# Gate and up projections: one low-half weight tile per chunk made by ScalarE and an accumulating DMA instead of VectorE

## Chip, cores and metric

The kernel runs on one core of one Trainium2 chip. The metric is device time in microseconds (us) from start to end of one execution. Three runs of the kernel before gave 1091.05, 1091.73 and 1091.93 us, a median of 1091.73 us. The execution that the profile shows is another one: it took 1091.39 us, of which 1089.6 us are the span from the first to the last instruction of the program; the other 1.79 us lie around it.

## What is computed

The reference is an encoder trunk of two layers on 256 tokens of width 1024, all in float32. One layer:

```
x = x + 0.5 * swiglu(rms_norm(x, ffn1_norm), w_gate, w_up, w_down)      # ffn 1
h = rms_norm(x, mix_norm);  z = h @ w_in                                # mix: two attention branches
x = x + merged(attention branches, gates) @ w_out
x = x + 0.5 * swiglu(rms_norm(x, ffn2_norm), w_gate, w_up, w_down)      # ffn 2

def swiglu(x, w_gate, w_up, w_down):
    return (silu(x @ w_gate) * (x @ w_up)) @ w_down
```

The hidden width of the feed-forward part (ffn) is 2816. There are four ffn in all, two in each layer, and each has its own weights.

## The kernel before

**Float32 accuracy by halves.** TensorE multiplies in a reduced format (`fp32r`). To keep float32 accuracy, each operand is split in a high half, which is the value rounded to fp32r, and a low half, which is the value minus the high half. A product is then three matmuls into the same PSUM bank: high by high, high by low and low by high. `three` (L167) issues them, on L168, L169 and L170: the second one is the first to read the low half of the weights.

**How weights arrive.** `load` (L137) takes a tile `raw` of 128 partitions by 1024 float32 (512 KB), issues a DMA for it on SyncE's queue (L140) and calls `parts` (L131), which takes a tile `wh` and a tile `wl` and lets `split_to` (L181) fill them: ScalarE copies `raw` to `wh` with the type fp32r (L182), then VectorE subtracts `wh` from `raw` into `wl` (L183). Three rings hold these tiles: `raw` has 4 buffers (RAW), `wh` and `wl` have 6 each (RING). A buffer is free again when its last reader is done: a `raw` after VectorE's subtraction, a `wh` or a `wl` after the last matmul that reads it.

**Gate and up.** The weights of gate and up lie interleaved, so that a chunk of 512 columns holds 256 gate columns and the 256 up columns that belong to them. `ffn` (L305) goes over 11 chunks (`NFC`, L434). For each, `columns` (L143) loads four tiles, each with two blocks of 128 rows out of the 1024 rows of the weights; the fourth tile holds the last 256 rows. Then, for each of the two halves `t` of the tokens, `project` (L270) runs 8 times `three`, that is 24 matmuls of 512 columns, over the four tiles in order. After it ScalarE takes the silu of the gate half (L447), VectorE multiplies it with the up half (`hh`, L449), and `defer` puts off the transposes of `hh` (`turn`, L312) for some matmuls. The first two chunks of the very first ffn are loaded in `opening` (L223) and are not made by the `columns` call of L441.

In a chunk, tile 4 is first read in the `t = 0` pass, after three quarters of its 24 matmuls, and last read at the end of the `t = 1` pass. With 6 buffers, a chunk's fourth `wl` takes the buffer of the second tile of the chunk before, if the buffers go round in turn; that one is given free halfway through the `t = 1` pass of the chunk before.

**Beside gate and up.** In chunks 2, 5 and 8, `prepare` (L357) builds sums of two rows of tiles for the down projection ahead of time: two more loads (L343), four subtractions (L347) and two more splits. `down` (L377) follows the 11 chunks, and after each first ffn of a layer stands `mix` (L470).

**Order of the work.** TensorE's order is written out by hand. The other engines' instructions are ordered at build time by the framework, from the program order and a simulated timeline, and each engine then runs its queue strictly in that order. GpSimd's queue (POOL) carries the reciprocal square roots of the norms (`rsqrt`, L172), the few loads of constants (L103 to L105, L461 to L468), and, in `mix` alone, attention work. The DMA issues of SyncE run on a queue of their own, in order.

Of the kernel before, what the change touches and what calls it, by code (L numbers as in the profile page):

```python
# [11 lines left out]
F32 = mybir.dt.float32  # L12
F32R = mybir.dt.float32r
I32 = mybir.dt.int32
BF16 = mybir.dt.bfloat16
AF = mybir.ActivationFunctionType
ALU = mybir.AluOpType
# [4 lines left out]
P = 128  # L22
D = 1024
# [4 lines left out]
KD = D // P  # L28
# [12 lines left out]
RING = 6  # L41
RAW = 4
# [14 lines left out]
def hybrid_encoder(ctx, tc, x, w_gu1, w_d1, w_in, b_gate, qk_gain, rpb, sink, t5,  # L57
                   w_bna, w_bsw, w_out, w_gu2, w_d2, c_mask, c_band, out):
    nc = tc.nc

    const = ctx.enter_context(tc.tile_pool(name="const", bufs=1))
    ring = ctx.enter_context(tc.tile_pool(name="ring", bufs=1))
# [68 lines left out]
    def parts(r, nk=2, n=512):  # L131
        wh = ring.tile([P, 2, 512], F32R, name="wh", tag="wh", bufs=RING)
        wl = ring.tile([P, 2, 512], F32R, name="wl", tag="wl", bufs=RING)
        split_to(wh[:, :nk, :n], wl[:, :nk, :n], r)
        return wh, wl

    def load(src, nk, n):  # L137
        raw = ring.tile([P, 2, 512], F32, name="raw", tag="raw", bufs=RAW)
        r = raw[:, :nk, :n]
        nc.sync.dma_start(r, src)  # L140
        return parts(r, nk, n)

    def columns(w, l, c0, n, nk=KD):  # L143
        return [load(w[l, 2 * i * P:(2 * i + 2) * P, c0:c0 + n].rearrange("(k p) n -> p k n", p=P), 2, n)
                for i in range(nk // 2)]

    def rows(w, l, k):
        return load(w[l, k * P:(k + 1) * P, :].rearrange("p (h n) -> p h n", h=2), 2, 512)
# [4 lines left out]
    def defer(lag, key, fn):  # L153
        later.append((now[0] + lag, len(later), key, fn))
        later.sort(key=lambda e: e[0])
# [25 lines left out]
    def split_to(hi, lo, src):  # L181
        linked("act", lambda: nc.scalar.activation(hi, src, AF.Copy))  # L182
        linked("dve", lambda: nc.vector.tensor_tensor(lo, src, hi.bitcast(F32), ALU.subtract))  # L183
# [39 lines left out]
    def opening(w, l):  # L223
        def piece(i, c=0):
            return load(w[l, 2 * i * P:(2 * i + 2) * P, c * 512:(c + 1) * 512].rearrange("(k p) n -> p k n", p=P),
                        2, 512)

        ps = [ps_g.tile([P, 512], F32, name="g", tag="g") for _ in range(T)]

        def steps(t, i):  # L230
            wh, wl = pieces[i]
            xh, xl = xT[t]
            for a, b in ((xh, wh), (xl, wh), (xh, wl)):
                for k in (2 * i, 2 * i + 1):
                    nc.tensor.matmul(ps[t], a[:, k, :], b[:, k % 2, :], start=a is xh and b is wh and k == 0,
                                     stop=b is wl and k == KD - 1)
            tick(2)

        pieces = []
        chain["act"] = warmed  # L240
        warmup(5)
        norm(0, 0, 0, True)
        pieces.append(piece(0))
        warmup(5)
        fetch(1, 0)
        norm(1, 0, 0, True)
        pieces.append(piece(1))
        fetch(0, 1)
        fetch(1, 1)
        warmup(3)  # L250
        steps(0, 0)
        norm(0, 0, 1, True)
        steps(1, 0)
        pieces.append(piece(2))
        norm(1, 0, 1, True)
        pieces.append(piece(3))
        square(0, 0, idle)
        square(0, 1, idle)
        second = [piece(0, 1)]
        square(1, 0, idle)  # L260
        square(1, 1, idle)
        second += [piece(i, 1) for i in range(1, KD // 2)]
        chain.clear()
        for i in (1, 2, 3):
            for t in range(T):
                steps(t, i)
        defer(24, "constants", constants)
        return ps, second

    def project(t, pieces, n):  # L270
        ps = ps_g.tile([P, 512], F32, name="g", tag="g")
        for k in range(KD):
            need(("norm", t, k // 4))
            xh, xl = xT[t]
            wh, wl = pieces[k // 2]
            three(ps[:, :n], xh[:, k, :], xl[:, k, :], wh[:, k % 2, :n], wl[:, k % 2, :n], k == 0, k == KD - 1)
            tick(n / 512)
        return ps
# [26 lines left out]
    def ffn(l, n, w_gu, w_d, after):  # L305
        with tc.tile_pool(name="ffn", bufs=1) as fp:
# [5 lines left out]
            def turn(c, t, hh):  # L312
                if t == 0:
                    tps[c] = ps_tp.tile([P, 4, P], F32, name="tp", tag="tp")
                tp = tps[c]
                for i in range(2):
                    nc.tensor.transpose(tp[:, SLOT[t][i], :], hh[:, i * P:(i + 1) * P], ident)  # L317
                if t < T - 1:
                    return
                m = 4 if PLAN[c] == "S" else 7  # L320
                hi = fp.tile([P, m, P], F32R, name=f"hi{m}", tag=f"hi{m}", bufs=NS if m == 7 else NFC - NS)
                lo = fp.tile([P, m, P], F32R, name=f"lo{m}", tag=f"lo{m}", bufs=NS if m == 7 else NFC - NS)
                if m == 7:
                    a = fp.tile([P, 8, P], F32, name="a", tag="sums", bufs=2)
                    nc.scalar.activation(a[:, :4, :], tp, AF.Copy)
                    for to, x, y, op in ((4, 0, 3, ALU.add), (6, 1, 0, ALU.subtract), (5, 4, 1, ALU.subtract),
                                         (7, 2, 5, ALU.subtract)):
                        nc.vector.tensor_tensor(a[:, to, :], a[:, x, :], a[:, y, :], op)
                    split_to(hi, lo, a[:, 1:, :])
                else:  # L330
                    with tc.high_priority(150 if c == NFC - 1 else 0):
                        split_to(hi, lo, tp)
                hs[c] = (hi, lo)
# [23 lines left out]
            def prepare(c):  # L357
                def into(name, r):
                    hl = [fp.tile([P, 2, 512], F32R, name=f"{name}{p}{c}", tag=f"{name}{p}{c}") for p in "hl"]
                    split_to(*hl, r)  # L360
                    return hl
                stored[c] = differences(block_row(2 * c), block_row(2 * c + 1), into)
# [71 lines left out]
            for c in range(NFC):  # L434
                first = n == 0 and c == 0
                if first:
                    both, second = opening(w_gu, l)
                elif n == 0 and c == 1:
                    pieces = second
                else:  # L440
                    pieces = columns(w_gu, l, c * 512, 512)  # L441
                if c in PREP:
                    prepare(PREP[c])
                for t in range(T):
                    ps = both[t] if first else project(t, pieces, 512)
                    sg = fp.tile([P, FC], F32, name="sg", tag="sg", bufs=2)
                    nc.scalar.activation(sg, ps[:, :FC], AF.Silu, scale=rstd[t])  # L447
                    hh = fp.tile([P, FC], F32, name="hh", tag="hh", bufs=2)
                    nc.vector.scalar_tensor_tensor(hh, ps[:, FC:], rstd[t], sg, op0=ALU.mult, op1=ALU.mult)  # L449
                    lag = LAST_LAG if (c, t) == (NFC - 1, T - 1) else H_LAG  # L450
                    defer(lag, ("h", c), lambda c=c, t=t, hh=hh: turn(c, t, hh))
# [294 lines left out]
    for l in range(L):  # L746
        ffn(l, 3 * l, w_gu1, w_d1, soon(3 * l + 1))
        mix(l, 3 * l + 1, soon(3 * l + 2))
        ffn(l, 3 * l + 2, w_gu2, w_d2, soon(3 * l + 3) if l + 1 < L else store)
# [78 lines left out]
```

## Time and profile before

| | us | share of the span |
|---|---|---|
| profiled execution | 1091.39 | |
| its span | 1089.6 | |
| TensorE (PE) busy | 1077.2 | 99% |
| VectorE (DVE) busy | 855.7 | 79% |
| ScalarE (ACT) busy | 658.7 | 60% |
| GpSimd (POOL) busy | 117.5 | 11% |
| subtractions into `wl`, L183, all 340 | 407.8 | |
| copies into `wh`, L182, all 340 | 348.9 | |

A row of the profile's groups reads: line, engine, operation, the tile written and the tiles read, the shapes, how many; then the busy time of all of them, the mean duration of one in nanoseconds; then the time that the engine sat idle just before them and what ended that. A row of a timeline reads: start and duration in us, engine, line, operation, tiles, shapes, how many were merged into the row; and in brackets the idle time before it and what ended it. A row of the DMA issues ends with the size in KB and the median time in us from the issue to the landing. In a row of the waits stand the total, the number of times and the longest, all in us where they are times. The ends of matmuls are modelled, so their starts are what tells of the pace.

### The profile page before, as it was taken

The numbers are of one execution on the slowest core, as the hardware profiler recorded it, in microseconds if no ns is written. First come the engines' busy times: TensorE is split into PE (matmuls) and PEld (weight loads), VectorE is DVE, ScalarE is ACT, GpSimd is POOL, SyncE is SP. The second block draws the span as 40 slices with busy tenths as digits, with TensorE's granted clock in tenths as the row PEclk, the third lists the DMA queues.
The fourth block names the chain that finished last, engine by engine and source line by source line (L and its number), as shares of the span: only waits on it lengthen the run. The fifth ranks groups of instructions, "written<-read, shape, count | busy, mean of one in ns | idle before, by whom it ended". The sixth has DMA issues, their size and how long they took to land.

```text
span 1089.6 us, 14660 instructions
## 1 busy us (share of the span) xinstructions
PE 1077.2 (99%) x5137; PEld 889.5 (82%) x5137; DVE 855.7 (79%) x1298; ACT 658.7 (60%) x1002; POOL 117.5 (11%) x118
## 2 busy tenths in 40 slices
PE   9999999999999999999999999999999999999998
PEld 7888878888888888888878888888888888888887
DVE  6887787889886778778777787788888767878785
ACT  6665654788764556565465565457877646656552
POOL 1400000243520000000000000003534000000000
PEclk9999999999999999999999999999999999999999
DMA  8876565755654676666657766557666555776661
GB/s 241 267 222 216 189 197 171 234 189 152 189 179 135 201 224 212 210 197 203 193 172 219 228 204 211 162 164 236 183 190 178 178 166 166 225 235 198 212 188 71
DMA packets 98827, 212.63 MB, mean 195 GB/s; under 512 B 7568, under 2 KB 13744, under 8 KB 98752
## 3 DMA queue, kind: packets, MB, share of 16 engines
q1 hardware_dynamic: 98560, 211.60, 62.1%
q8 instruction: 40, 0.66, 0.2%
q0 software_dynamic: 192, 0.08, 0.1%
q14 instruction: 35, 0.29, 0.1%
HBM read 210.59 MB, written 1.06 MB: 194 GB/s over the span
## 4 chain that ended last, share of the span: by engine, by line
PE 86%; DVE 8%; ACT 3%; issue 2%; DMA 2%; ACTq 0%; DVEq 0%
PE g L168 19%; PE g L170 19%; PE g L169 19%; PE acc L168 5%; PE acc L170 5%; PE acc L169 5%; DVE wl L183 3%; PE tp L317 2%; ACT wh L182 1%; PE tp L168 1%; PE tp L169 1%; PE tp L170 1%; PE pt L572 1%; DMA raw<-in_w_d 1%; PE sc L551 1%
## 5 line engine op out<-in xcount | busy, mean ns | idle before, releaser
L183 DVE TENSOR_TENSOR wl<-raw,wh 128x1024 fp32r<-128x1024 f32 (+1 forms) x340 | 407.8, 1216 | 68.8 <-ACT wh L182 67.5
L182 ACT ACTIVATE wh<-raw 128x1024 fp32r<-128x1024 f32 (+1 forms) x340 | 348.9, 1046 | 111.9 <-PE g L170 35.0
L168 PE MATMUL g<-wh,xh 128*128 128x512 f32 (+1 forms) x976 | 389.9, 399 | 0.0
L170 PE MATMUL g<-wh,xl 128*128 128x512 f32 (+1 forms) x976 | 379.0, 388 | 0.7 <-DVE xl L183 0.7
L169 PE MATMUL g<-wl,xh 128*128 128x512 f32 (+1 forms) x976 | 377.6, 387 | 0.4 <-DVE wl L183 0.4
L170 PEld LDWEIGHTS g<-wh,xl 128*128 128x128 f32 x976 | 183.4, 188 | 41.4 <-DVE xl L183 2.1
L169 PEld LDWEIGHTS g<-wl,xh 128*128 128x128 f32 x976 | 184.1, 189 | 32.0 <-DVE wl L183 0.8
L168 PEld LDWEIGHTS g<-wh,xh 128*128 128x128 f32 x976 | 183.6, 188 | 30.9 <-DVE hh L449 0.2
L447 ACT ACTIVATE sg<-g,rs_y 128x256 f32<-128x256 f32 x88 | 41.4, 471 | 117.1 <-PE g L170 116.8
L347 DVE TENSOR_TENSOR u<-raw 128x512 f32<-128x512 f32 x56 | 38.7, 691 | 61.9 <-DMA raw<-in_w_d 61.3
L168 PE MATMUL acc<-wh,hi 128*128 128x512 f32 x200 | 79.3, 396 | 0.0
L170 PE MATMUL acc<-wh,lo 128*128 128x512 f32 x200 | 78.0, 390 | 0.0
L169 PE MATMUL acc<-wl,hi 128*128 128x512 f32 x200 | 77.9, 390 | 0.0
L174 POOL TENSOR_TENSOR rs_y<-ms,mhalf 128x1 f32<-128x1 f32 x12 | 6.7, 556 | 660.3 <-DVE ms L220 651.9
L449 DVE SCALAR_TENSOR_TENSOR hh<-g,rs_y,sg 128x256 f32<-128x256 f32 x88 | 42.2, 480 | 38.8 <-ACT sg L447 38.7
L182 ACT ACTIVATE corner<-raw 128x512 fp32r<-128x512 f32 x28 | 17.6, 630 | 54.7 <-DMA raw<-in_w_d 38.4
L564 POOL TENSOR_TENSOR S<-S,sm 128x512 f32<-128x512 f32 x32 | 37.2, 1161 | 71.4 <-DVE sm L563 45.2
L170 PEld LDWEIGHTS acc<-wh,lo 128*128 128x128 f32 x200 | 37.6, 188 | 8.1
L169 PEld LDWEIGHTS acc<-wl,hi 128*128 128x128 f32 x200 | 37.6, 188 | 7.4
L168 PEld LDWEIGHTS acc<-wh,hi 128*128 128x128 f32 x200 | 37.6, 188 | 7.4
L557 ACT ACTIVATE S<-S,mx 128x256 f32<-128x256 f32 x64 | 32.0, 501 | 7.4 <-DVE mx L554 7.4
L317 PEld LDWEIGHTS tp<-ident,hh 128*128 128x128 f32 x176 | 24.2, 140 | 14.1 <-DVE hh L449 3.4
(190 smaller groups left out, 1477.3 us busy)
## 6 DMA issues: line engine op xcount, KB each, us to landing
raw<-in_w_gu SPq DMA_DIRECT2D x176, 512.0 KB, 4.4
raw<-in_w_d SPq DMA_DIRECT2D x100, 512.0 KB, 4.3
raw<-in_w_in SPq DMA_DIRECT2D x64, 512.0 KB, 4.3
raw<-in_w_out SPq DMA_DIRECT2D x16, 512.0 KB, 3.6
bb<-in_b_gate SPq DMA_DIRECT2D x16, 256.0 KB, 3.5
raw<-in_w_bsw SPq DMA_DIRECT2D x8, 512.0 KB, 4.0
raw<-in_w_bna SPq DMA_DIRECT2D x8, 512.0 KB, 3.5
raw<-in_w_d SPq DMA_DIRECT2D x12, 256.0 KB, 2.6
```

The lines of the kernel that those rows point to most:

```text
L168: nc.tensor.matmul(ps, xh, wh, start=first, stop=False)
L169: nc.tensor.matmul(ps, xh, wl, start=False, stop=False)
L170: nc.tensor.matmul(ps, xl, wh, start=False, stop=last)
L182: linked("act", lambda: nc.scalar.activation(hi, src, AF.Copy))
L183: linked("dve", lambda: nc.vector.tensor_tensor(lo, src, hi.bitcast(F32), ALU.subtract))
L317: nc.tensor.transpose(tp[:, SLOT[t][i], :], hh[:, i * P:(i + 1) * P], ident)
L347: sub = lambda to, x, y: nc.vector.tensor_tensor(to, x, y, ALU.subtract)
L447: nc.scalar.activation(sg, ps[:, :FC], AF.Silu, scale=rstd[t])
L449: nc.vector.scalar_tensor_tensor(hh, ps[:, FC:], rstd[t], sg, op0=ALU.mult, op1=ALU.mult)
L551: nc.tensor.matmul(ps[:, t, :], qT[:, h, t * P:(t + 1) * P], k[:, kidx(h), :], start=i == 0, stop=i == 1)
L557: nc.scalar.activation(S_[:, t, :], S_[:, t, :], AF.Exp, bias=mx[:, t:t + 1], scale=-1.0, accum_out=sm[:, t:t + 1])
L564: nc.gpsimd.tensor_tensor(S_, S_, sm.unsqueeze(2).to_broadcast([P, T, S]), ALU.mult)
```

## The change

A new function `summed` loads a tile as `load` does, on SyncE's queue, but fills the two halves in another way: ScalarE first writes minus the rounded value to `wl` (a copy with scale -1 into fp32r), then the rounded value to `wh`; then a DMA issued on GpSimd's queue reads the same 512 KB of raw weights from DRAM a second time and adds them to what stands in `wl`. What results is raw minus high, as before. VectorE has no part in it.

```
+    def summed(src):
+        raw = ring.tile([P, 2, 512], F32, name="raw", tag="raw", bufs=RAW)
+        nc.sync.dma_start(raw, src)
+        wh = ring.tile([P, 2, 512], F32R, name="wh", tag="wh", bufs=RING)
+        wl = ring.tile([P, 2, 512], F32R, name="wl", tag="wl", bufs=RING)
+        nc.scalar.activation(wl, raw, AF.Copy, scale=-1.0)
+        nc.scalar.activation(wh, raw, AF.Copy)
+        nc.gpsimd.dma_start(wl, src, accum_op=ALU.add)
+        return wh, wl
+
@@ in ffn, the loop over chunks
                 else:
-                    pieces = columns(w_gu, l, c * 512, 512)
+                    pieces = columns(w_gu, l, c * 512, 512, KD - 2)
+                    pieces.append(summed(w_gu[l, D - 2 * P:, c * 512:(c + 1) * 512].rearrange("(k p) n -> p k n", p=P)))
```

`columns` with `KD - 2` loads the first three tiles of the chunk as before. The fourth comes from `summed`, in 9 chunks of the first ffn and in all 11 of the other three: 42 tiles in all.

## The prediction

> **What bounds the kernel now.** I read the page's busy times first, then what TensorE waited for, then one long stretch of gate and up alone.
>
> ```profile
> span 1089.6 us, 14660 instructions
> PE 1077.2 (99%) x5137; PEld 889.5 (82%) x5137; DVE 855.7 (79%) x1298; ACT 658.7 (60%) x1002; POOL 117.5 (11%) x118
> ```
>
> ```profile
> PE tp L317 <- DVE hh L449: 1.2, 3, 0.6
> PE g L170 <- DVE xl L183: 0.7, 1, 0.7
> PE g L169 <- DVE wl L183: 0.4, 1, 0.4
> ```
>
> ```profile
> 367.00:490.00 123.00, 123.00 (x560) 100.30 (x559) 93.23 (x130) 72.75 (x97) 0.56 (x1) 1.00 0.67 213
> ```
>
> The last row is chunks 0 to 10 of the second ffn of layer 0; its columns are the stretch, its length, then the busy time of PE, PEld, DVE, ACT and POOL, the granted clock, the share of the DMA engines and GB/s. TensorE is busy in all 123.00 us, at full clock, while VectorE has 29.77 us free. That "busy" is modelled, so I checked it against starts (rows further down): 415.42, 415.64 and 415.19 lie 0.22 to 0.23 us apart, and this pace holds through the stretch. So TensorE's own stream sets the end, and VectorE sets it only in the few places of the waits: the rows above (2.3 us) and those of its weight loads:
>
> ```profile
> PEld tp L317 <- DVE hh L449: 3.4, 5, 1.0
> PEld g L170 <- DVE xl L183: 2.1, 5, 1.1
> ```
>
> All five together, counted as if none overlapped, are 7.8 us. That is the most that less work on VectorE can give back here.
>
> **What the change takes away.** 42 subtractions:
>
> ```profile
> L183 DVE TENSOR_TENSOR wl<-raw,wh 128x1024 fp32r<-128x1024 f32 x43 | 51.5, 1220 | 5.0 <-ACT wh L182 5.0
> L182 ACT ACTIVATE wh<-raw 128x1024 fp32r<-128x1024 f32 x43 | 44.6, 1055 | 11.2 <-DMA raw<-in_w_gu 6.5 <-PE g L170 4.2 <-ACT vh L182 0.2
> ```
>
> These are the groups of the same stretch. 42 x 1.22 = 51 us leave VectorE, and 42 x 1.06 = 44 us come to ScalarE. Neither lies on the path by itself: VectorE has the 29.77 us free, and ScalarE goes in this stretch from 72.75 to 72.75 + 11 x 1.06 = 84.4 us of 123. What matters is the time at which a tile's low half is there.
>
> **The window for one low half.** A typical chunk, the fifth of that ffn, on ScalarE, VectorE and TensorE:
>
> ```profile
> 408.14 0.94 ACT L182 ACTIVATE hi<-a 128x896 fp32r<-128x896 f32 x1
> 408.98 2.00 ACT L182 ACTIVATE wh<-raw 128x1024 fp32r<-128x1024 f32 x2
> 411.26 0.48 ACT L447 ACTIVATE sg<-g,rs_y 128x256 f32<-128x256 f32 x1 [0.29 <-PE g L170]
> ```
>
> ```profile
> 410.41 2.35 DVE L183 TENSOR_TENSOR wl<-raw,wh 128x1024 fp32r<-128x1024 f32 x2
> ```
>
> ```profile
> 411.20 0.48 PE L168 MATMUL g<-wh,xh 128*128 128x512 f32 x1
> ...
> 415.19 0.39 PE L170 MATMUL g<-wh,xl 128*128 128x512 f32 x1
> 415.42 0.39 PE L168 MATMUL g<-wh,xh 128*128 128x512 f32 x1
> 415.64 0.39 PE L169 MATMUL g<-wl,xh 128*128 128x512 f32 x1
> ```
>
> The chunk's first matmul starts at 411.20, the first three tiles make 18, so the fourth tile begins at 415.42 and its low half is first read at 415.64. ScalarE's copy for that tile begins at 408.98; it can't begin much earlier, since the buffers come free only about then (the L447 row shows the chunk before ending just ahead of 411.26, and the buffer is freed by the second of its last four tiles), and the 0.94 us copy at 408.14 stands before it. VectorE's subtraction is done 1.22 us into its row, at 411.63: 4.0 us early.
>
> After the change ScalarE's negative copy takes that first place: 408.98 + 1.06 = 410.04. Only then may GpSimd issue the DMA. To be in time it must land within 415.64 - 410.04 = 5.6 us. The tightest of the 42 chunks is the first of the third ffn:
>
> ```profile
> 548.57 2.94 ACT L182 ACTIVATE wh<-raw 128x1024 fp32r<-128x1024 f32 x3
> ```
>
> ```profile
> 553.44 0.39 PE L169 MATMUL g<-wl,xh 128*128 128x512 f32 x1
> ```
>
> There it is 553.44 - 548.57 - 1.06 = 3.8 us. The same two starts, read for each of the 42 tiles, give 3.8 to 6.0 us with a mean of 5.4; chunks 0, 2, 5 and 8, where norms or `prepare` crowd ScalarE, are the short ones. A late tile isn't made up for: the stall lies at three eighths of a chunk, the next chunk's buffer is freed at three quarters, so each chunk pays (landing minus window) anew.
>
> **How long the DMA takes.** No row of the trace shows an accumulating DMA; these are nearest:
>
> ```profile
> raw<-in_w_gu SPq DMA_DIRECT2D x176, 512.0 KB, 4.4
> raw<-in_w_out SPq DMA_DIRECT2D x16, 512.0 KB, 3.6
> mask<-in_c_mask POOLq DMA_DIRECT2D x1, 32.0 KB, 2.0
> qkg<-in_qk_gain POOLq DMA_DIRECT2D x1, 4.0 KB, 2.5
> snk<-in_sink POOLq DMA_DIRECT2D x1, 8.0 KB, 5.2
> vec<-in_c_band POOLq DMA_DIRECT2D x1, 16.0 KB, 4.9
> table<-in_t POOLq DMA_DIRECT2D x1, 1.0 KB, 5.4
> vec_d<-vec POOLq DMA_DIRECT2D x1, 16.0 KB, 3.9
> ```
>
> ```profile
> q1 hardware_dynamic: 98560, 211.60, 62.1%
> ```
>
> ```profile
> 21.31 0.79 POOL L103 DMA_DIRECT2D qkg<-in_qk_gain  x1
> 23.71 0.52 POOL L462 DMA_DIRECT2D table<-in_t  x1
> ```
>
> One pass of 512 KB (0.524 MB) over all 16 engines costs 0.621 x 1089.6 / 211.60 x 0.524 = 1.7 us. Two estimates. From SyncE's loads: 4.4 us issue to landing, 0.5 for GpSimd's longer issue (its rows show 0.52 to 0.79), and one more pass, because the sum must also read what stands in `wl`: 4.4 + 0.5 + 1.7 = 6.6. From GpSimd's loads: they hold next to no data and yet took 2.0 to 5.4 us, mean 4.0, while other loads were under way; with two passes, 4.0 + 3.4 = 7.4. I take 7.0, between them. Bounds: 3.6, as SyncE's quickest row of that size (nothing hidden in it for a gain: it is a load with no sum), and 5.4 + 3 x 1.7 = 10.5, GpSimd's slowest with read, read and write one after the other.
>
> That the sum reads twice isn't shown by any row. The Trainium skill, Collectives: The Full Stack, section "The bandwidth ceiling: the fold count and why AG ≠ RS ≠ AR", says that a reduction in the DMA path needs two reads for one write, and that this, not the adding, halves its rate. No run here shows it so far; without the second pass the two estimates would be 4.9 and 5.7, about 5.3, just under the mean window, and only the short windows would lose, some 6 us in sum.
>
> **The sum.** 42 x (7.0 - 5.4) = 67 us of stalls on TensorE. By the bounds: at 3.6 us none, since even the tightest window is 3.8; at 10.5 us 42 x 5.1 = 214. The rest comes to nothing. ScalarE's added copy pushes the following `wh` and the silu row (411.26) by 1.06 us; the next user of the silu's bank comes a pass of 24 matmuls later, 24 x 0.228 = 5.5 us, and `wh` itself is there at 411.1 for 415.42. If that cover were gone, it would be 1.06 us a chunk, 45 us. On GpSimd's queue nothing stands behind the waiting DMA in gate and up: POOL is busy 0.56 us in the 123, one reciprocal root at the ffn's start. SyncE's queue keeps its order, and its fourth `raw` is now freed by ScalarE at 411.1, before the 411.63 of VectorE. The 42 extra loads raise the share of the DMA engines from 0.67 by 2 x 1.7 / 11.2 per chunk (123 / 11 = 11.2 us) to 0.97 before the chunks stretch, and to about 0.85 with 1.6 us more in each: close, but not over. VectorE's relief I take as nothing here, as a TensorE that waits each chunk for a DMA gives VectorE's late places time anyway. Against the profiled execution: 1091.4 + 67 = 1158 us; that execution is within 0.4 us of the median of the three runs, so I leave it.
>
> **Rivals.** *The DMA lands in time, and VectorE's relief shows.* Place: the ends of `down` and the heads of the ffn, where the five rows above wait. Price: up to -7.8, half of it likely, so about 1087.5, at the least 1083.6. It decides for a landing time below some 4.5 us, where only the tightest few windows lose. For it: 3.6 and 4.4 us of SyncE's loads, and a VectorE at 93.23 of 123. Against: GpSimd's rows, four of six at 3.9 or more with no data. The Trainium skill, DMA: Bandwidth & Descriptors, section "Anatomy of one DMA — SWDGE (gpsimd) path", gives a fit of 2.0 us plus the bytes at 436 GB/s, which is an estimate of 3.2 us here and would put this rival first; the trace's 2.0 to 5.4 us for nearly empty ones disagrees under load.
>
> *Hidden, and nothing gained.* Landing at 4.5 to 5.4 us: the short ones of the 42 windows lose 1 to 8 us in sum, VectorE's relief gives some back, 1090 to 1095 around no change. For it: windows at 5.6 in most chunks.
>
> *The sum is slow in the engines.* If an adding pass costs several plain ones, landing is at 9 us and the loss 42 x 3.6 = 151, 1243 us; with two passes in the engine's time for reading and more for the sum, the 0.67 share would go past 1 and the plain loads come late too. Nothing in the trace speaks against it but that all loads there are plain.
>
> *The change doesn't do what it says.* The build orders ScalarE's queue anew; if the negative copies were put behind later copies, the window shrinks by 1.06 us or two for the same landing, 45 to 90 us more. That stays mostly inside the range; the rows speak neither way.
>
> **How the numbers follow.** Forecast, landing at 5.5 to 8.8 us: 0.55. Copies put late: 0.03. Slow sum, above that: 0.18, its upper half beyond 1243. Hidden without gain: 0.14. Hidden with gain: 0.10. A measurement of this kernel tells about 0.2% from no change, 2.2 us. Faster by that: 0.10. Within it: 0.13, the most of the hidden case without gain. Slower: 0.77, the forecast, the late copies, the slow sum and 0.01 of the rest. The range runs from 1090, which leaves out the gain, to 1243, which leaves out the slow sum's upper half: 0.19 outside. The forecast's own range is 1096 (landing 5.5) to 1234 (8.8).
>
> **What would show it.** Right: 42 rows of the DMA on GpSimd's queue with 6.5 to 7.5 us to landing; TensorE waiting 42 times at L169 for a DMA into `wl`, 1 to 2 us each, and a chunk of some 12.8 instead of 11.2 us; VectorE's subtraction rows down by 42; a DMA share near 0.85. Wrong in size: the same waits, another landing time. Wrong in kind: no waits at L169 (hidden), or waits there for ScalarE or for plain loads instead of the sum.

## The result and the profile after

The changed kernel took 1308.72 us (median of four runs, 1302.92 to 1309.87) against 1091.62 us (median of four) of the kernel before. The ratio is 1.1976, with a 95% interval of 1.1961 to 1.1990. The profiled execution took 1309.02 us, 217.6 us more than that of before. Lines of `kernel.py` are 10 or 11 higher than before: `three` is now L178 to L180, `split_to` L192 and L193, the new function L148 to L150.

The page of the changed kernel: busy times, granted clock by slice, the groups of the new DMA and of the second matmul, the DMA queues and the issues.

```profile
span 1307.2 us, 14713 instructions
PE 1141.5 (87%) x5137; PEld 926.1 (71%) x5137; DVE 814.6 (62%) x1256; ACT 695.0 (53%) x1044; POOL 162.1 (12%) x160
PEclk9889899999999999999988988999999998999899
...
q1 hardware_dynamic: 98560, 211.60, 51.3%
q0 software_dynamic: 11616, 22.10, 9.8%
...
L179 PE MATMUL g<-wl,xh 128*128 128x512 f32 (+1 forms) x976 | 403.8, 414 | 155.7 <-DMA wl<-in_w_gu 155.0
...
L150 POOL DMA_DIRECT2D wl<-in_w_gu x42 | 50.5, 1202 | 581.8 <-ACT wl L148 507.7
...
raw<-in_w_gu SPq DMA_DIRECT2D x176, 512.0 KB, 5.5
...
wl<-in_w_gu POOLq DMA_DIRECT2D x42, 512.0 KB, 8.5
```

VectorE has 41 us less to do and ScalarE 36 more. TensorE, which had stood at 99%, is at 87%, and the waits name one cause: the second matmul of `three`, 155.0 us for the DMA into `wl`. But TensorE's busy time also grew, from 1077.2 to 1141.5 us, for the same 5137 matmuls. That is the second loss: the granted clock, a mean of 1.000 before, is 0.952.

The waits of TensorE alone confirm the count; the columns are total, times, longest.

```profile
PE g L179 <- DMA wl<-in_w_gu: 155.0, 42, 7.9
```

One typical chunk, on ScalarE, GpSimd and TensorE:

```profile
463.67 1.04 ACT L148 ACTIVATE wl<-raw 128x1024 fp32r<-128x1024 f32 x1
464.62 1.04 ACT L149 ACTIVATE wh<-raw 128x1024 fp32r<-128x1024 f32 x1
```

```profile
465.12 1.20 POOL L150 DMA_DIRECT2D wl<-in_w_gu  x1 [18.63 <-ACT wl L148]
```

```profile
470.30 0.39 PE L178 MATMUL g<-wh,xh 128*128 128x512 f32 x1
473.41 0.50 PE L179 MATMUL g<-wl,xh 128*128 128x512 f32 x1 [2.73 <-DMA wl<-in_w_gu]
```

ScalarE's negative copy ends at 464.71. GpSimd starts the DMA 0.41 us later and spends 1.20 us issuing it. The matmul that needs it could have started at 470.53, 5.8 us after the copy; it starts at 473.41. That is the window of the prediction and a landing that doesn't fit in it.

The chunk before it, where the wait was longer, and two stretches of it with the granted clock in the column behind POOL's:

```profile
450.17 0.39 PE L178 MATMUL g<-wh,xh 128*128 128x512 f32 x1
456.34 0.79 PE L179 MATMUL g<-wl,xh 128*128 128x512 f32 x1 [5.79 <-DMA wl<-in_w_gu]
456.93 0.63 PE L180 MATMUL g<-wh,xl 128*128 128x512 f32 x1
457.36 0.63 PE L178 MATMUL g<-wh,xh 128*128 128x512 f32 x1
457.79 0.63 PE L179 MATMUL g<-wl,xh 128*128 128x512 f32 x1
```

```profile
450.40:456.20 5.80, 0.16 (x1) 0.00 (x0) 0.29 (x1) 0.00 (x0) 0.00 (x0) 0.92 1.06 302
456.20:459.50 3.30, 3.16 (x9) 2.47 (x10) 0.05 (x1) 0.56 (x2) 0.00 (x0) 0.50 0.13 51
```

After the wait the matmuls start 0.43 us apart instead of 0.23, at a clock of 0.50. Read over all 42 waits from the starts of matmuls: the gaps sum to 161.7 us (3.85 each), and after 32 of them 6 to 12 matmuls run at the half pace, 50.7 us in all. Together 212.4 of the 217.6 us. This accounting is from one trace; the experiments test its parts.

### The profile page after: what moved, and what is told of

The parts are those of the page before. It is cut to its first block, busy times and chain, and to the rows that moved or that the text cites. A ratio compares the mean times of both kernels' runs of the same rounds, so it can differ in the third digit from the quotient of the medians.

```text
span 1307.2 us, 14713 instructions
## 1 busy us (share of the span) xinstructions
PE 1141.5 (87%) x5137; PEld 926.1 (71%) x5137; DVE 814.6 (62%) x1256; ACT 695.0 (53%) x1044; POOL 162.1 (12%) x160
## 3 DMA queue, kind: packets, MB, share of 16 engines
q1 hardware_dynamic: 98560, 211.60, 51.3%
q0 software_dynamic: 11616, 22.10, 9.8%
HBM read 232.61 MB, written 1.06 MB: 179 GB/s over the span
## 4 chain that ended last, share of the span: by engine, by line
PE 44%; issue 34%; DMA 11%; DVE 4%; ACT 4%; POOL 3%; POOLq 0%; ACTq 0%; DVEq 0%
DMA wl<-in_w_gu 10%; PE g L179 7%; PE g L180 7%; PE g L178 7%; PE acc L180 5%; PE acc L178 5%; PE acc L179 5%; POOL wl L150 2%; ACT wh L192 1%; DVE wl L193 1%; PE tp L180 1%; PE tp L178 1%; PE tp L179 1%; PE pt L583 1%; PE sc L562 1%
## 5 line engine op out<-in xcount | busy, mean ns | idle before, releaser
L179 PE MATMUL g<-wl,xh 128*128 128x512 f32 (+1 forms) x976 | 403.8, 414 | 155.7 <-DMA wl<-in_w_gu 155.0
L193 DVE TENSOR_TENSOR wl<-raw,wh 128x1024 fp32r<-128x1024 f32 (+1 forms) x298 | 359.5, 1215 | 137.4 <-ACT wh L192 136.3
L178 PE MATMUL g<-wh,xh 128*128 128x512 f32 (+1 forms) x976 | 409.5, 420 | 0.0
L180 PE MATMUL g<-wh,xl 128*128 128x512 f32 (+1 forms) x976 | 397.8, 408 | 0.0
L192 ACT ACTIVATE wh<-raw 128x1024 fp32r<-128x1024 f32 (+1 forms) x298 | 306.7, 1042 | 124.8 <-PE g L180 65.5
L180 PEld LDWEIGHTS g<-wh,xl 128*128 128x128 f32 x976 | 195.5, 200 | 41.6
L178 PEld LDWEIGHTS g<-wh,xh 128*128 128x128 f32 x976 | 196.2, 201 | 35.4 <-DVE hh L460 0.2
L150 POOL DMA_DIRECT2D wl<-in_w_gu x42 | 50.5, 1202 | 581.8 <-ACT wl L148 507.7
L178 PE MATMUL acc<-wh,hi 128*128 128x512 f32 x200 | 79.2, 396 | 0.0
L180 PE MATMUL acc<-wh,lo 128*128 128x512 f32 x200 | 78.0, 390 | 0.0
L192 ACT ACTIVATE corner<-raw 128x512 fp32r<-128x512 f32 x28 | 17.6, 628 | 58.2 <-DMA raw<-in_w_d 28.8
L149 ACT ACTIVATE wh<-raw 128x1024 fp32r<-128x1024 f32 x42 | 43.9, 1046 | 1.8 <-PE g L180 1.8
L148 ACT ACTIVATE wl<-raw 128x1024 fp32r<-128x1024 f32 x42 | 43.9, 1046 | 0.4 <-PE g L180 0.2
L180 PEld LDWEIGHTS acc<-wh,lo 128*128 128x128 f32 x200 | 37.6, 188 | 8.1
```

The lines of the kernel that those rows point to most:

```text
L148: nc.scalar.activation(wl, raw, AF.Copy, scale=-1.0)
L149: nc.scalar.activation(wh, raw, AF.Copy)
L150: nc.gpsimd.dma_start(wl, src, accum_op=ALU.add)
L178: nc.tensor.matmul(ps, xh, wh, start=first, stop=False)
L179: nc.tensor.matmul(ps, xh, wl, start=False, stop=False)
L180: nc.tensor.matmul(ps, xl, wh, start=False, stop=last)
```

## Experiments

The theory: the loss is (landing minus window) in each of the 42 chunks, plus a clock that falls after a long wait. Rivals: the added traffic and GpSimd's descriptors cost by themselves; ScalarE's copies do; the slow matmuls come from loads that bunch up.

**The sum or the path.** A plain load in place of the sum:

```
-        nc.gpsimd.dma_start(wl, src, accum_op=ALU.add)
+        nc.gpsimd.dma_start(wl, src)
```

> The DMA on GpSimd's queue overwrites the low half with the raw weights instead of adding them, so the values are others; all waits stay. If the second read is what makes the sum slow (2 KB packets of 176 ns in the changed kernel against 84 ns of plain loads, 16 rows an engine, so 1.5 us), the landing falls from 8.5 to about 7.0 us, the stalls from 3.85 to about 2.4 us, with few half-clock phases left: about 1200 us. If the path makes it slow (GpSimd's issue of 1.2 us, sharing the engines with the plain loads), the landing stays above 8 us and the time at 1285 to 1310.

1208.37 us in one run. Its page:

```profile
q1 hardware_dynamic: 98560, 211.60, 54.9%
q0 software_dynamic: 11616, 22.10, 6.6%
...
wl<-in_w_gu POOLq DMA_DIRECT2D x42, 512.0 KB, 7.2
```

The landing fell from a mean of 8.7 to 7.0 us. Of these 1.7 us, 0.48 are GpSimd's own: it issues the plain load in 0.72 us, the sum in 1.20. In the engines one DMA took 0.066 x 1206.5 / 42 = 1.9 us, against 0.098 x 1307.2 / 42 = 3.05 with the sum. TensorE's waits fell to 88.5 us (39 times), and the slowed matmuls, after 11 waits instead of 32, to about 20. So adding, instead of overwriting, is worth about 100 us here, two thirds of it as shorter waits and the rest as clock that they no longer cost. That the extra time in the engines is a second read is not shown: the queue's row counts 22.10 MB with the sum and without. And a plain load from GpSimd's queue in this place is still 116 us too slow.

**The clock.** Matmuls whose results nothing reads, ahead of the fourth tile in the `t = 0` pass of the 42 chunks:

```
...
+            if keep and t == 0 and k == KD - 2:
+                for _ in range(16):
+                    nc.tensor.matmul(keep[0], xh[:, 0, :], pieces[0][0][:, 0, :], start=True, stop=True)
...
```

> 16 matmuls whose results nothing reads fill 3.65 us of each of the 42 waits. If the other 55 us of the loss are TensorE's halved clock after each wait, the clock stays at 1.00 and the time is 1091.6 + 42 x 3.9, about 1255 to 1265 us. If the slow matmuls have another cause (the loads that bunch up after a wait), they stay and the time is at or above 1300.

1281.47 us in one run, between the two. Its waits:

```profile
PE g L179 <- DMA wl<-in_w_gu: 25.3, 15, 4.5
```

The sum works out: 42 x 3.65 = 153 us of filler, 25 of waits that were longer than the filler, and about 10 of slowed matmuls after 6 of those, on 1092.2 of the kernel before, run beside it: 1281. The mean clock is 0.991. Where the filler covers the wait, no slow matmul follows, though the same loads run; the bunched loads are out as a cause. The expected 1255 to 1265 took every wait for the mean one.

**The window, by buffers.** The same six `wl` buffers, split in two for the fourth tiles and four for the others (outside gate and up every third tile takes from the two):

```
-        wl = ring.tile([P, 2, 512], F32R, name="wl", tag="wl", bufs=RING)
+        wl = ring.tile([P, 2, 512], F32R, name="wl", tag="ws", bufs=2)
         nc.scalar.activation(wl, raw, AF.Copy, scale=-1.0)
...
+        other = pick and turn_of[0] % 3 == 0
+        wl = ring.tile([P, 2, 512], F32R, name="wl", tag="ws" if other else "wl", bufs=2 if other else RING - 2)
```

> The fourth tiles' low halves get two buffers of their own out of the same six, so that ScalarE's negative copy need not wait for the matmuls of the chunk before. If the loss is landing minus window, it goes: 1084 to 1096 us, the lower end if VectorE's relief is worth something. If the added 22 MB and GpSimd's descriptors are what costs, it stays well above 1110.

1187.45 us, ratio 1.0883 (1.0852 to 1.0913): better by 121 us, and far from hidden. Its waits and its DMA:

```profile
ACT wl L152 <- DMA raw<-in_w_gu: 116.4, 39, 6.7
...
PE g L183 <- DMA wl<-in_w_gu: 53.6, 13, 6.6
...
PE tp L331 <- DVE hh L464: 13.0, 9, 2.1
```

```profile
wl<-in_w_gu POOLq DMA_DIRECT2D x42, 512.0 KB, 6.1
```

With no buffer to wait for, the build put the negative copy so early in ScalarE's queue that it stands there waiting for its raw load, 116.4 us in all, and holds the copies and silus behind it; TensorE's waits for `hh` grow from 1.2 us in the kernel before to 13.0. 29 of 42 sums are now in time; 13 are still late, by 53.6 us, and the clock falls again after 11 waits (some 21 us). In 11 of the 13 the negative copy had itself waited 1.1 to 2.3 us for its raw load. The window theory holds for the 29; the expectation missed that ScalarE's queue is in order and its head would wait. This run also shows the sum on a quieter DMA: where less than 0.75 of a plain tile's bytes moved during a sum (28 of 42), it landed in 6.0 us on average; in the changed kernel 2.3 or more moved along with nearly every sum, and the mean was 8.7. (A slower sum also has more time for others to move, so this does not measure what each tile costs it.)

**The window, by order.** The original buffers, and the matmuls of a chunk as three tiles for `t = 0`, two for `t = 1`, the fourth for `t = 0`, the rest for `t = 1`. The same order was put into the kernel before:

```
-                for t in range(T):
-                    ps = both[t] if first else project(t, pieces, 512)
...
+                for t, k0, k1 in ((0, 0, 6), (1, 0, 4), (0, 6, KD), (1, 4, KD)):
...
+                        ps = banks[t] = project(t, pieces, 512, k0, k1, banks[t])
...
```

> The same matmuls in another order: the first three tiles for t = 0, the first two for t = 1, then the fourth for t = 0 and the rest for t = 1. The window for the low half grows from 5.4 to some 9.6 us against the 8.9 that the DMA needs with its start. Landing minus window: 1088 to 1105 us, no wait of more than 1 us in most chunks. Traffic or descriptors: above 1150.

> The kernel before (low halves from VectorE) with the matmul order of e5_order. It tells how much of the 63 us that e5_order still loses is the order's own. If the order costs (in e5_order TensorE waits 28.9 us for VectorE's hh, since the second bank is done two tiles before the next chunk), the time is 1115 to 1135; if the rest is the added DMA's, it is 1090 to 1100.

With the sum 1155.56 us, ratio 1.0579 (1.0552 to 1.0605); with VectorE's low halves 1129.46 us, ratio 1.0350 (1.0332 to 1.0368). TensorE's waits in the first and in the second of the two:

```profile
PE g L178 <- DVE hh L467: 28.9, 27, 2.6
PE g L179 <- DMA wl<-in_w_gu: 13.8, 12, 4.0
```

```profile
PE g L168 <- DVE hh L456: 23.4, 16, 2.4
```

The order costs 38 us by itself, as the second expectation had it, mostly since the PSUM banks now come free too late. Against that base the sum costs 26 us, not 217: a window that was meant to be 4 us longer takes 88% of the loss away, and the clock is at 0.997 in the profiled run (0.984 to 0.997 in the four). The first expectation was too low, as it left out the order's own price; taken alone, 1155.56 lies where it had put a cost of traffic or descriptors (above 1150), and only the second run shows that most of the loss is the order's.

**What VectorE's relief is worth, and what ScalarE's copy costs.** First, no low half is made for the fourth tile and the third tile's (`prior`) is read in its place; second, the negative copy stays and the DMA goes. Both against the changed kernel:

```
...
-        wl = ring.tile([P, 2, 512], F32R, name="wl", tag="wl", bufs=RING)
-        nc.scalar.activation(wl, raw, AF.Copy, scale=-1.0)
         nc.scalar.activation(wh, raw, AF.Copy)
-        nc.gpsimd.dma_start(wl, src, accum_op=ALU.add)
-        return wh, wl
+        return wh, prior
...
```

```
-        nc.gpsimd.dma_start(wl, src, accum_op=ALU.add)
```

> The low half of each fourth tile isn't made at all: its matmuls read the third tile's low half, so the products are others, the work on TensorE is the same, and VectorE has its 51 us less with no copy and no DMA in exchange. This is the most that the change could have gained. TensorE bound: 1089 to 1092. VectorE's late places worth something: down to 1084.

> ScalarE's negative copy stays, the adding DMA is left out, so the low half holds minus the high half and the products are others. If ScalarE's 44 us lie beside other work, the time is 1088 to 1094, like e7_relief. If the copies delay the next tiles and the silu, it is up to 45 us more, about 1136.

The first took 1090.25 us, ratio 0.9987 (0.9978 to 0.9996): with 42 subtractions gone and nothing in exchange, 1.4 us are won. The second took 1092.37 us, ratio 1.0005 (0.9996 to 1.0014): ScalarE's copies cost nothing that can be told, and the loss is the DMA's.

**The added traffic by itself.** To make room, the sums that `prepare` builds in chunk 8 were moved to `down` (`PREP` without `8: 5`); then the adding DMA went into a tile that nothing reads:

```
+    spare = ring.tile([P, 2, 512], F32R, name="spare", tag="spare", bufs=1)
...
+        wh, wl = parts(raw)
+        nc.scalar.activation(spare[:, 0, :8], raw[:, 0, :8], AF.Copy, scale=-1.0)
+        nc.gpsimd.dma_start(spare, src, accum_op=ALU.add)
+        return wh, wl
```

> The kernel before with the sums of the third prepared chunk (PREP without 8: 5) made in the down stage instead, which frees 16 KB a partition: the base for e11_traffic. Between 1091 and 1110, since VectorE then has more to do in down.

> e10_base plus the 42 adding DMAs, into a tile that nothing reads; the low halves come from VectorE as before. No matmul waits for the sum. If the added transfers cost nothing by themselves, it is e10_base within 3 us, and the whole loss of the change is the wait for the sum. If they make the plain loads late, it is 20 to 90 us above e10_base, and TensorE waits for halves whose raw tile landed late.

The base took 1092.15 us, ratio to the kernel before 1.0002 (0.9993 to 1.0011). With the traffic it was 1101.55 us, ratio 1.0086 (1.0069 to 1.0102). In the base:

```profile
raw<-in_w_gu SPq DMA_DIRECT2D x176, 512.0 KB, 4.5
```

```profile
PE tp L317 <- DVE hh L449: 1.1, 4, 0.4
```

In the second:

```profile
raw<-in_w_gu SPq DMA_DIRECT2D x176, 512.0 KB, 5.0
spare<-in_w_gu POOLq DMA_DIRECT2D x42, 512.0 KB, 6.0
```

```profile
ACT spare L150 <- DMA raw<-in_w_gu: 155.3, 40, 5.4
...
PE tp L328 <- DVE hh L461: 7.0, 8, 1.8
```

So 42 sums that no matmul waits for cost 9.4 us, at a landing of 6.0; the plain loads take 5.0 instead of 4.5 us, and VectorE's late places grow. That is between the two expectations, and 4% of the change's loss. It isn't the price of traffic alone: each sum comes with a small copy on ScalarE, which stands at the head of that queue until the raw load has landed, 155.3 us in all, and once, for 5.4 us, until the sum before it had left `spare`; one of the eight waits for `hh` (1.1 us) follows that one. How the 9.4 us divide stays open. Together they are several times the 1.4 us that VectorE's relief is worth, so that even sums hidden entirely would be likely to lose; no run shows that.

## Why the prediction was wrong

**What bounds the kernel** was right: TensorE, with VectorE in a few places. So was the place of the loss: 42 waits at the second matmul for the new DMA, and a slower kernel. The prediction allowed VectorE's relief at most 7.8 us and took it as nothing; it is 1.4.

**The windows** were right. The prediction read 3.8 to 6.0 us, mean 5.4. In the changed kernel, from the end of the negative copy to the time at which the matmul could have started, they are 5.36 us on average, with one of 1.9 and the rest from 3.7 to 6.3. From the copy's end to GpSimd's start pass 0.46 us on average (0.41 in the median chunk), and with the 8.70 of landing 42 x (9.16 - 5.36) gives 160 us; TensorE's gaps sum to 161.7.

**How long the DMA takes** was the mis-sized term: 7.0 was predicted from the copy's end, 9.2 measured. The 1.7 us for a second read look well sized, as the plain load landed 1.7 us sooner, but that is partly luck: only 3.05 - 1.9 = 1.15 us of it are in the engines, and 0.48 are the longer issue. The Trainium skill, Collectives: The Full Stack, section "The bandwidth ceiling: the fold count and why AG ≠ RS ≠ AR", says that the second read is what a reduction in the DMA path costs; the 3.05 us against 1.9 in the engines agree in direction, though this pair gives a factor of 1.6 and not its two. Too small were the rest: GpSimd's issue takes 1.20 us for this tile, not 0.5, which came from loads of 32 KB and less; the start after the copy, 0.46, wasn't in the sum; and the sum runs beside some three plain tiles of the next chunk, whose buffers come free about then, and lands in 8.7 instead of the 6.0 of a quiet DMA. Mis-sizing by 2.2 us is 42 x 2.16 = 91 us.

**"The rest comes to nothing"** was the step that failed outright. It held for ScalarE (ratio 1.0005) and for GpSimd's queue. The added traffic, put at "close, but not over" and priced at nothing, is at most about 9.4 us, as far as the run with the sums that no matmul waits for tells; the share of the DMA engines, forecast near 0.85, is 51.3 + 9.8 = 61% of the span, but 1.06 in the 5.80 us of the wait shown above, so the average hid how the loads bunch beside a sum. And the list had no line for the clock: the prediction noted that TensorE ran "at full clock" and let it stay there while putting 42 waits into its stream. The half-clock matmuls after 32 waits are 51 us of the loss, and the filler experiment shows that it is the waiting that brings them. 67 + 91 + 51 is 209 of the 218 us. The range's upper end of 1243 assumed a landing of 9 us without that term; with it the same landing would lead past 1290, by these sums.

**The rivals.** Hidden sums, with or without gain: wrong, 42 waits. The slow sum: the landing of 9.2 from the copy's end lies just inside its range, but not for its reason: adding takes the engines 1.6 times a plain load from the same queue, not several. The copies put late: not so, as the windows show. The Trainium skill, DMA: Bandwidth & Descriptors, section "Anatomy of one DMA — SWDGE (gpsimd) path", gives a fit by which 512 KB would need an estimated 3.2 us; no DMA of that size on GpSimd's queue landed in under 4.9 us here, the plain load's quickest.

## What to carry to other kernels

Before a step on the way to a busy TensorE is moved to a DMA, compare its landing under the loads of that very moment with the time from buffer release to first use; spare time elsewhere doesn't help, since each round pays anew. Price a wait that recurs in a TensorE-bound stream with the clock that it may cost, not by its length alone. And first leave the work out: a ceiling of 1.4 us told more about relieving VectorE than its 79%.

## What the runs showed of the hardware

After many of TensorE's waits the granted clock is 0.50, and some 6 to 14 matmuls start 0.43 us apart: after 32 of 42 waits with a mean of 3.85 us, and after 11 of 36 (those over 1.2 us), with a mean of 2.55, in the run with plain loads. Length alone doesn't decide it: in the changed kernel one wait of 3.66 us passed without and one of 2.65 us didn't, and with plain loads one of 2.07 us didn't. What decides it is how the wait lies. In every trace here the clock changes only on a raster of 3.41 us, and a stretch at 0.50 lasts one or two steps of it. These steps of the changed kernel hold the wait of 3.66 us (the first two) and that of 2.65 us (the third); after the length stands TensorE's busy time, and behind POOL's the clock:

```profile
154.95:158.36 3.41, 1.71 (x8) 1.09 (x6) 0.20 (x1) 0.00 (x0) 0.00 (x0) 1.00 1.06 247
158.36:161.78 3.42, 1.62 (x8) 1.35 (x9) 0.00 (x0) 0.15 (x1) 0.00 (x0) 1.00 0.75 280
...
172.02:175.43 3.41, 1.11 (x5) 0.93 (x6) 0.18 (x1) 0.00 (x0) 0.00 (x0) 1.00 1.06 335
175.43:178.84 3.41, 3.41 (x11) 2.64 (x10) 3.13 (x6) 2.00 (x4) 0.00 (x0) 0.50 0.38 123
```

The longer wait leaves TensorE idle for 1.7 and 1.8 us of two steps, the shorter one for 2.3 us of one, and after that one the clock falls. Over the eleven traces it fell after all 58 steps at full clock with more than 1.92 us idle, after none of 3510 with less than 1.76, and after 7 of the 17 between. (The first 12 and the last 6 us of each trace are left out; this is read from the clock's records, and no experiment moved a wait along the raster.) The Trainium skill, TensorE: Matmul & The Clock Gate, section "Part 1: The HAM clock gate (the "warmup" mystery)", has the clock halved after an idle window of 3.4 us that runs free of the kernel. The clock of 0.50 and the raster of 3.41 us fit it; but here a window that was idle for a little over half was enough, and the measurement decides.

An accumulating DMA of 512 KB from GpSimd's queue lands in 5.8 us at the quickest and in up to 11.0 beside plain loads, with 1.20 us of it spent on GpSimd; a plain one of that size from the same queue in 4.9 to 8.6 us, with 0.72.
